# The S5 preparation rebuilt: tables from coarse times fine angles, K_n products issued together, their tile zeroed once, inputs loaded a tile ahead

## The chip, the cores and the metric

The kernel runs on one core of one Trainium2 chip. The metric is the device time of one execution in microseconds (us). Engines are named as in the profile: PE is TensorE's matmul, DVE is VectorE, ACT is ScalarE, POOL is GpSimd, SP is SyncE, which here only issues DMA transfers.

## The reference, cut to what matters

One step of a decoder of four layers on 256 prompt tokens and 8 samples of 4 tokens, 1024 features. Every layer has a token mixer and a squared-ReLU MLP. Layers 0 and 3 mix by a spatial gating unit, layer 1 by an RG-LRU, layer 2 by an S5 state-space layer:

```
h = rmsnorm(x, norm_mix[layer])
x = x + mixer(h)                                     # layer 0: gating unit, 1: RG-LRU, 2: S5
x = x + square(relu(rmsnorm(x, norm_ffn[layer]) @ w_ff1)) @ w_ff2
# S5, 64 groups of 16 features and 64 complex states:
ab = exp(lam * dt)                                   # lam = lam_re + i lam_im, dt = exp(log_dt)
bb = (ab - 1) / lam * B
x_t = ab * x_(t-1) + bb u_t ;  y_t = Re(C x_t) + d_skip * u_t ;  out = glu(gelu(y))
```

## The kernel before

Activations stay on chip as tiles of 128 features by 288 tokens. Every float32 product runs as three passes over split operands, weights whi and wlo against xh and xl (lines 273 to 275). The weights come as 176 chunks of 1 MB (`raw`), 44 per layer: 12 for the mixer of layer 0 (chunks 0 to 11), 32 for its MLP (12 to 43), and so on. A chunk is loaded by SP (line 179), split by ACT (whi, line 202) and DVE (wlo, line 203), and used on PE by 16 products of each of the three lines. Three raw buffers and three split buffers let the loads run some four chunks ahead. Each engine takes its instructions in order, and SP its DMA issues; a tile framework fixes that order at build time by priorities and by its own idea of times.

The S5 layer needs matrices that depend on weights alone. They are made while layers 0 and 1 run, as a list of background tasks that `spare` takes one by one, at a priority 300 steps later than their place. `s5_params` computes a, its powers (pw), q = (a − 1)/lambda, the cosines and sines of the angle times 4, 8 .. 128 (rc, rs), and a^(3−l) q (qq). `s5_spread` transposes qq on PE through two PSUM banks of the kind `sec` (there are three) and stores it to DRAM (qd). Then, for each of eight u tiles m, six tasks: `s5_inputs` twice (bi, on POOL, from bt and the spread qb), `s5_powers` twice (cn, on DVE), `s5_table` (tab, on POOL, 64 cosines and sines by doubling, 26 instructions), and `s5_kernels` (bq on DVE; eight small products into pk on PE, line 881; the copies of their blocks into the zeroed tile kt on ACT). Results go to DRAM (scr) and are fetched in layer 2. The tasks of four tiles run beside the MLP of layer 0, those of the other four beside that of layer 1. Within the mixer of layer 0, the tasks above `n_tasks` run while the u half of its first product is made:

```
def spare(upto=0):
    if len(background) > (upto or 0):
        with tc.high_priority(offset=-PRI_SPARE):
            background.pop(0)(state['bg'])
```

In the gating unit of layer 0 the rows after the u chunks are, for each of eight g: mixing products into a `sec` bank on PE (lines 508, 509), a scaled sum q on DVE (line 511), y = q * u on POOL (line 513), its split yh on ACT and yl on DVE (lines 269, 270), and then the output product.

## Time and profile before

| | |
|---|---|
| median of three runs | 1320.63 us (1314.42 to 1326.06) |
| profiled execution, span from the first to the last instruction | 1312.3 us; what lies around the span is not recorded |
| PE busy | 1266.0 us |
| mean granted clock of PE | 0.981 |
| HBM read and written | 214.17 and 14.60 MB |

PE is the engine with the most busy time; DVE is busy for 926.8 us, ACT for 617.9, POOL for 376.4. A busy PE isn't PE at its peak, since the ends of matmuls are modelled. Idle time of an engine matters only where another waits for it.

### The profile page before, as it was taken

The numbers are of one execution on the slowest core, as the hardware profiler recorded it, in microseconds if no ns is written. First come the engines' busy times: TensorE is split into PE (matmuls) and PEld (weight loads), VectorE is DVE, ScalarE is ACT, GpSimd is POOL, SyncE is SP. The second block draws the span as 40 slices with busy tenths as digits, with TensorE's granted clock in tenths as the row PEclk, the third lists the DMA queues.
The fourth block names the chain that finished last, engine by engine and source line by source line (L and its number), as shares of the span: only waits on it lengthen the run. The fifth ranks groups of instructions, "written<-read, shape, count | busy, mean of one in ns | idle before, by whom it ended". The sixth has DMA issues, their size and how long they took to land.

```text
span 1312.3 us, 23910 instructions
## 1 busy us (share of the span) xinstructions
PE 1266.0 (96%) x9802; PEld 1223.4 (93%) x9802; DVE 926.8 (71%) x1437; ACT 617.9 (47%) x1019; POOL 376.4 (29%) x524
## 2 busy tenths in 40 slices
PE   8999999799979998999999999999999999999997
PEld 7999999699968997998999899999999999999997
DVE  8899759686787897748768756655666677655653
ACT  5745532354564644236443345534544645534541
POOL 2237647501258485860121200000012221000010
PEclk9999999899988998999999999999999999999998
DMA  8526666555431767546567434554446334544431
GB/s 290 207 97 205 225 185 220 181 197 194 145 121 62 232 214 243 185 153 217 182 241 257 159 131 159 177 176 162 161 161 217 135 133 160 190 161 160 161 129 37
DMA packets 47006, 230.33 MB, mean 176 GB/s; under 512 B 7904, under 2 KB 13712, under 8 KB 24368
## 3 DMA queue, kind: packets, MB, share of 16 engines
q1 hardware_dynamic: 38016, 209.63, 46.5%
q0 software_dynamic: 8016, 18.45, 4.4%
q8 instruction: 77, 1.26, 0.4%
q10 hardware_dynamic: 864, 0.72, 0.2%
q14 instruction: 33, 0.27, 0.1%
HBM read 214.17 MB, written 14.60 MB: 174 GB/s over the span
## 4 chain that ended last, share of the span: by engine, by line
PE 63%; POOL 14%; DMA 9%; DVE 8%; issue 2%; ACT 2%; SPq 0%; DVEq 0%; POOLq 0%; ACTq 0%
PE acc L275 19%; PE acc L273 19%; PE acc L274 19%; DMA qb<-qd 6%; DMA scr<-tab 3%; POOL tab L905 2%; DVE wlo L203 2%; POOL ta L903 2%; POOL tab L904 2%; POOL bi L836 2%; POOL tb L903 1%; POOL bt L837 1%; POOL bi L838 1%; PE sec L959 1%; PE sec L881 1%
## 5 line engine op out<-in xcount | busy, mean ns | idle before, releaser
L202 ACT ACTIVATE whi<-raw 128x1024 fp32r<-128x1024 f32 (+1 forms) x354 | 363.6, 1048 | 330.9 <-PE acc L274 267.0
L203 DVE TENSOR_TENSOR wlo<-raw,whi 128x1024 fp32r<-128x1024 f32 (+1 forms) x354 | 443.4, 1269 | 106.4 <-ACT whi L202 104.6
L273 PE MATMUL acc<-xh,whi 128*128 128x288 f32 x1472 | 442.3, 301 | 8.0 <-ACT whi L202 7.1
L275 PE MATMUL acc<-xh,wlo 128*128 128x288 f32 x1472 | 440.1, 300 | 7.1 <-DVE wlo L203 7.0
L274 PE MATMUL acc<-xl,whi 128*128 128x288 f32 x1472 | 434.4, 295 | 2.1 <-DVE xl L285 2.1
L273 PE MATMUL acc<-hh,whi 128*128 128x288 f32 x1024 | 305.5, 298 | 3.9 <-ACT hh L269 3.9
L274 PE MATMUL acc<-hl,whi 128*128 128x288 f32 x1024 | 304.7, 298 | 1.1 <-DVE hl L270 1.1
L275 PE MATMUL acc<-hh,wlo 128*128 128x288 f32 x1024 | 303.2, 296 | 0.0
L273 PEld LDWEIGHTS acc<-xh,whi 128*128 128x128 f32 x1472 | 278.6, 189 | 12.5 <-ACT whi L202 8.1
L275 PEld LDWEIGHTS acc<-xh,wlo 128*128 128x128 f32 x1472 | 277.7, 189 | 11.8 <-DVE wlo L203 10.1
L274 PEld LDWEIGHTS acc<-xl,whi 128*128 128x128 f32 x1472 | 282.2, 192 | 5.9 <-DVE xl L285 3.4
L297 POOL TENSOR_TENSOR ss<-ss,sq 128x288 f32<-128x288 f32 x62 | 67.7, 1092 | 566.5 <-ACT sq L296 566.0
L273 PEld LDWEIGHTS acc<-hh,whi 128*128 128x128 f32 x1024 | 192.6, 188 | 7.3 <-ACT hh L269 4.7
L274 PEld LDWEIGHTS acc<-hl,whi 128*128 128x128 f32 x1024 | 192.9, 188 | 4.5 <-issue 2.6
L275 PEld LDWEIGHTS acc<-hh,wlo 128*128 128x128 f32 x1024 | 193.6, 189 | 2.4 <-issue 2.2
L411 DVE TENSOR_TENSOR t<-acc,r 128x288 f32<-128x288 f32 x64 | 29.1, 455 | 138.8 <-PE acc L275 138.8
L269 ACT ACTIVATE hh<-t 128x288 fp32r<-128x288 f32 x128 | 56.9, 444 | 125.6 <-DVE t L394 125.6
L270 DVE TENSOR_TENSOR hl<-t,hh 128x288 fp32r<-128x288 f32 x128 | 63.3, 495 | 25.8 <-ACT hh L269 24.4
L394 DVE TENSOR_TENSOR t<-t 128x288 f32<-128x288 f32 x128 | 64.8, 506 | 4.7 <-ACT t L388 4.7
L388 ACT ACTIVATE t<-acc 128x288 f32<-128x288 f32 x128 | 51.0, 398 | 21.8 <-PE acc L275 18.1
L285 DVE SCALAR_TENSOR_TENSOR xl<-x,aux,xh 128x288 fp32r<-128x288 f32 x64 | 52.9, 834 | 7.3 <-ACT xh L284 7.3
L284 ACT ACTIVATE xh<-x,aux 128x288 fp32r<-128x288 f32 x64 | 33.5, 527 | 33.9 <-DVE x L519 15.5
(324 smaller groups left out, 1508.1 us busy)
## 6 DMA issues: line engine op xcount, KB each, us to landing
raw<-in_wall SPq DMA_DIRECT2D x173, 1024.0 KB, 4.8
sci<-scr SPq DMA_DIRECT2D x8, 768.0 KB, 6.3
sco<-scr SPq DMA_DIRECT2D x8, 768.0 KB, 5.6
bt<-in_bt POOLq DMA_DIRECT2D x8, 512.0 KB, 7.7
scr<-cn SPq DMA_DIRECT2D x8, 512.0 KB, 5.0
qb<-qd POOLq DMA_DIRECT2D x8, 512.0 KB, 13.4
scr<-bi POOLq DMA_DIRECT2D x8, 512.0 KB, 6.1
raw<-in_wall SPq DMA_DIRECT2D x4, 512.0 KB, 8.9
```

The costliest lines, as they stand in the source:

```text
L202: nc.scalar.activation(h[:, c], self.raw[i][:, c], AF.Copy)
L203: nc.vector.tensor_tensor(l[:, c], self.raw[i][:, c], h[:, c].bitcast(F32), op=OP.subtract)
L269: S.activation(h, src, AF.Copy)
L270: V.tensor_tensor(l, src, h.bitcast(F32), op=OP.subtract)
L273: PE.matmul(ps, wh, h, start=first, stop=False)
L274: PE.matmul(ps, wh, l, start=False, stop=False)
L275: PE.matmul(ps, wl, h, start=False, stop=last)
L285: V.scalar_tensor_tensor(xl[k], x[k], A[g][:, k:k + 1], xh[k].bitcast(F32), op0=OP.mult, op1=OP.subtract)
L297: G.tensor_tensor(state['ss'], state['ss'], q, op=OP.add)
L388: i = S.activation(q, ps[:, :T], AF.Relu)
L394: V.tensor_tensor(q2, q, q, op=OP.mult)
L903: eng.tensor_tensor(t[:, :, :, :w], tab[:, :, :, :w], fb, op=OP.mult)
```

## The change

The diff also strips the comments from the file, so that line numbers move (L881 becomes L909, L513 becomes L515). What is left, cut to its core:

```diff
-  ... ('rc', [6, 32]), ('rs', [6, 32]), ('pw', [5, 3, 32]), ('q', [2, 32]), ('qq', [4, 32, 2])
+  ... ('fine', [2, 32, 8]), ('coarse', [2, 32, 8]), ('pw', [5, 3, 32]), ('q', [2, 32])
 def s5_params(pool):
...
-        V.tensor_copy(s5['rs'].rearrange('p n i -> p (n i)'), sn[:, 64:])
-        V.tensor_copy(s5['rc'].rearrange('p n i -> p (n i)'), cs[:, 64:])
+        rc, rs = (v[:, 64:].rearrange('p (n i) -> p n i', n=6) for v in (cs, sn))
+        fine, coarse = s5['fine'], s5['coarse']
+        G.tensor_copy(fine[:, 0, :, 0], rc[:, 0])
+        G.tensor_copy(fine[:, 1, :, 0], rs[:, 0])
+        G.memset(coarse[:, 0, :, 0], 1.0)
+        G.memset(coarse[:, 1, :, 0], 0.0)
+        ta, tb = (pool.tile([P, 2, 32, 4], F32, name=f's5d{i}') for i in range(2))
+        for tab, first in ((fine, 0), (coarse, 3)):
+            for n in range(3):
+                w = 2 ** n
+                for t, f in ((ta, rc), (tb, rs)):
+                    G.tensor_tensor(t[:, :, :, :w], tab[:, :, :, :w], f[:, first + n][:, None, :, None].to_broadcast([P, 2, 32, w]), op=OP.mult)
+                G.tensor_tensor(tab[:, 0, :, w:2 * w], ta[:, 0, :, :w], tb[:, 1, :, :w], op=OP.subtract)
+                G.tensor_tensor(tab[:, 1, :, w:2 * w], ta[:, 1, :, :w], tb[:, 0, :, :w], op=OP.add)
+    def s5_loads(m):
+        four = slice(4 * m, 4 * m + 4)
+        bt, qb = bg_([P, 2, 4, P], 'bt', 2), bg_([P, 4, 2, P], 'qb', 2)
+        cc, bs = bg_([P, 2, 4, 32], 'cc', 2), bg_([P, 2, 4, 32], 'bs', 2)
+        nc.sync.dma_start(qb...)      # the same transfers; bt and qb were issued by POOL,
+        nc.sync.dma_start(bt, ...)    # cc and bs by SP in s5_powers and s5_kernels
+        nc.sync.dma_start(cc, ...)
+        nc.sync.dma_start(bs, ...)
+        s5['in', m] = bt, qb, cc, bs
 def s5_inputs(m, n, eng):
         if n == 0:
+            if m == 0 or m == KT // 2:
+                s5_loads(m)
+                s5['kt'] = bg_([P, 4, P], 'kt')
+                G.memset(s5['kt'], 0.0)
...
 def s5_powers, s5_kernels:      # the stores of cn and kt
-            nc.sync.dma_start(s5['scr'][m][:, 1536:2560]..., cn...)
+            G.dma_start(s5['scr'][m][:, 1536:2560]..., cn...)
-        nc.sync.dma_start(s5['scr'][m][:, 2560:3072], ...kt)
+        G.dma_start(s5['scr'][m][:, 2560:3072], ...kt)
 def s5_kernels(m, eng):
-        for n in range(2):
+        lead = None
+        for n in (1, 0):
             for q in range(4):
-                PE.matmul(pk[32 * q:32 * q + 32, :P], bq[:, n, q], cn[:, n, 0:4, q], start=n == 0, ...)
+                with ExitStack() as stay:
+                    if lead is not None:
+                        stay.enter_context(tc.high_priority())
+                        stay.enter_context(tc.issue_after(lead.ins))
+                    i = PE.matmul(pk[32 * q:32 * q + 32, :P], bq[:, n, q], cn[:, n, 0:4, q], start=n == 1, ...)
+                lead = lead or i
-        kt = bg_([P, 4, P], 'kt')
-        G.memset(kt, 0.0)
+        kt = s5['kt']
...
-            S.activation(kt[s, :, s], pk[s, :P]..., AF.Copy)
+            # blocks 1 and 3 so on ACT; blocks 0 and 2 by V.tensor_copy on DVE
 def s5_table(m, eng):            # six instructions in place of 26
+        for c in range(2):
+            fine = s5['fine'][:, c, four][:, :, None].to_broadcast([P, 4, 8, 8])
+            for t, n in ((ta, 0), (tb, 1)):
+                step = s5['coarse'][:, n, four][:, :, :, None].to_broadcast([P, 4, 8, 8])
+                eng.tensor_tensor(t[:, c]..., fine, step, op=OP.mult)
+        eng.tensor_tensor(tab[:, 0], ta[:, 0], tb[:, 1], op=OP.subtract)
+        eng.tensor_tensor(tab[:, 1], ta[:, 1], tb[:, 0], op=OP.add)
-        n_tasks[0] = 6 * KT + 1
+        n_tasks[0] = 6 * KT
-  lambda p, m=m_: s5_inputs(m, 0, G)
+  lambda p, m=m_: (s5_inputs(m, 0, G), (m + 1) % (KT // 2) and s5_loads(m + 1))
```

With `n_tasks` one lower, `s5_spread` now runs in the mixer of layer 0 with `s5_params`, and not in the MLP.

What stands where in a row is shown at three places. First, PE in the MLP of layer 0, at the K_n products of the second tile of 128 (`sec<-cn,bq`; the main products of the MLP are `acc<-xh,whi` and the like). Before:

```order
L275 MATMUL acc_2928<-xh_95,wlo_2809 128x288
L881 MATMUL sec_2532<-cn_2237,bq_2524 32x128
L273 MATMUL acc_2928<-xh_96,whi_2808 128x288
L881 MATMUL sec_2532<-cn_2237,bq_2524 32x128
L274 MATMUL acc_2928<-xl_104,whi_2808 128x288
L881 MATMUL sec_2532<-cn_2237,bq_2524 32x128
L275 MATMUL acc_2928<-xh_96,wlo_2809 128x288
```

Now:

```order
L275 MATMUL acc_2834<-xh_97,whi_2740 128x288
L276 MATMUL acc_2834<-xl_105,whi_2740 128x288
L909 MATMUL sec_2468<-cn_2193,bq_2460 32x128 x8
L277 MATMUL acc_2834<-xh_97,wlo_2741 128x288
L275 MATMUL acc_2834<-xh_98,whi_2740 128x288
```

The eight products of a tile, which alternated with the main products, stand in one run; all eight tiles read so now.

Second, the gating unit of layer 0, where its u chunks end and its mixing begins. PE before (`vT`: the transposed v; `wr`, `wrs`: the mixing weights):

```order
L274 MATMUL acc_1029<-xl_106,whi_953 128x288
L275 MATMUL acc_1029<-xh_98,wlo_954 128x288
L508 MATMUL sec_1106<-wr_218,vT 128x128
L508 MATMUL sec_1106<-wr_219,vT 128x128
L509 MATMUL sec_1106<-wrs,vT 128x32
```

PE now (`s5qq` is what `s5_spread` transposes):

```order
L276 MATMUL acc_1067<-xl_106,whi_991 128x288
L277 MATMUL acc_1067<-xh_98,wlo_992 128x288
L833 MATMUL sec_981<-ident,s5qq 128x128
L833 MATMUL sec_986<-ident,s5qq 128x128
L510 MATMUL sec_1144<-wr_217,vT 128x128
L510 MATMUL sec_1144<-wr_218,vT 128x128
L511 MATMUL sec_1144<-wrs,vT 128x32
```

The two transposes of the spread stand ahead of the first mixing product. POOL at the same place before (`ss<-ss,sq` adds up the squares of the norm, L513 is y):

```order
L466 TENSOR_TENSOR ss_304<-ss_304,sq_555 128x288
L466 TENSOR_TENSOR ss_304<-ss_304,sq_572 128x288
L492 DMA out_vs<-vo 32x1024
L513 TENSOR_TENSOR t_77_1112<-t_1110,u_221 128x288
L513 TENSOR_TENSOR t_80_1122<-t_1120,u_222 128x288
```

POOL now, the last of the new instructions (L784 and the lines about it are `fine` and `coarse`):

```order
L784 TENSOR_TENSOR s5coarse<-s5d_812,s5d_813 128x32x2
L782 TENSOR_TENSOR s5d_812<-s5coarse,s5w_789 128x256
L782 TENSOR_TENSOR s5d_813<-s5coarse,s5w_788 128x256
L783 TENSOR_TENSOR s5coarse<-s5d_812,s5d_813 128x32x4
L784 TENSOR_TENSOR s5coarse<-s5d_812,s5d_813 128x32x4
L515 TENSOR_TENSOR t_79_1150<-t_1148,u_220 128x288
```

The 26 instructions of the two tables' parts stand ahead of the first y (L515, formerly L513).

Third, SP's queue in the MLP of layer 0. `raw` are the weight chunks: `raw_1672` before and `raw_1719` now are chunk 18, `raw_1749` and `raw_1794` chunk 19. Before:

```order
L179 DMA raw_1587<-in_wall 128x2048
L847 DMA cc_2678<-in_cc 128x2x128
L863 DMA scr_114<-cn_1742 128x2x512
L179 DMA raw_1672<-in_wall 128x2048
L179 DMA raw_1749<-in_wall 128x2048
L871 DMA bs_2993<-in_bs 128x2x128
L179 DMA raw_1824<-in_wall 128x2048
```

Now:

```order
L848 DMA bs_1631<-in_bs 128x2x128
L844 DMA qb_2116<-qd 128x1x1024
L181 DMA raw_1719<-in_wall 128x2048
L846 DMA bt_2115<-in_bt 128x2x512
L844 DMA qb_2549<-qd 128x1x1024
L181 DMA raw_1794<-in_wall 128x2048
L847 DMA cc_2117<-in_cc 128x2x128
L846 DMA bt_2548<-in_bt 128x2x512
L181 DMA raw_1869<-in_wall 128x2048
```

The loads of qb for tiles 2 and 3 of 128 (`qb_2116`, `qb_2549`) stand ahead of chunks 18 and 19 in one queue; in the MLP of layer 1 two such loads stand ahead of chunks 63 and 65.

## Rows read from the trace of the kernel before

**Rows 1.** The page's first part: busy time of each engine, its share and instructions.

```profile
PE 1266.0 (96%) x9802; PEld 1223.4 (93%) x9802; DVE 926.8 (71%) x1437; ACT 617.9 (47%) x1019; POOL 376.4 (29%) x524
```

**Rows 2.** Windows, L273 alone: window, length, PE, PEld, granted clock, DMA share, GB/s.

```profile
104.00:337.90 233.90, 154.08 (x513) 97.19 (x513) 0.98 0.60 197
440.90:674.40 233.50, 153.85 (x513) 96.84 (x513) 0.99 0.60 197
801.40:1005.90 204.50, 151.66 (x513) 96.13 (x513) 1.00 0.48 166
...
104.00:150.50 46.50, 33.17 (x112) 1.00 0.65 219
```

**Rows 3.** Timeline of PE, start and duration: single L881, then a run with five.

```profile
610.85 0.29 PE L275 MATMUL acc<-xh,wlo 128*128 128x288 f32 x1
611.08 0.41 PE L881 MATMUL sec<-cn,bq 128*32 128x128 f32 x2
...
616.44 0.29 PE L273 MATMUL acc<-xh,whi 128*128 128x288 f32 x1
...
572.79 0.40 PE L275 MATMUL acc<-xh,wlo 128*128 128x288 f32 x1
573.12 0.62 PE L881 MATMUL sec<-cn,bq 128*32 128x128 f32 x10
...
573.91 0.30 PE L274 MATMUL acc<-xl,whi 128*128 128x288 f32 x1
```

**Rows 4.** Waits of PE: who waited for what; us in total, times, longest.

```profile
PE acc L273 <- ACT whi L202: 9.2, 3, 6.6
PE acc L275 <- DVE wlo L203: 7.6, 12, 1.2
PE acc L273 <- ACT hh L269: 3.9, 3, 1.9
```

**Rows 5.** Timelines of ACT and POOL about 250 us; in brackets the wait ahead.

```profile
253.27 1.11 ACT L887 ACTIVATE kt<-sec 32x128 f32<-32x128 f32 x4 [11.87 <-POOL kt L884]
...
244.09 1.29 POOL L836 TENSOR_TENSOR bi<-bt,qb 128x512 f32<-128x512 f32 x1 [5.58 <-DMA qb<-qd]
```

**Rows 6.** Window behind that wait: length, PE busy, clock, DMA share, GB/s.

```profile
255.80:262.00 6.20, 5.78 (x22) 0.50 0.57 187
```

**Rows 7.** Groups of POOL by form: busy, mean ns, idle time before.

```profile
L836 POOL TENSOR_TENSOR bi<-bt,qb 128x512 f32<-128x512 f32 x16 | 25.0, 1563 | 56.3 <-DMA qb<-qd 56.3
L903 POOL TENSOR_TENSOR ta<-tab,s5rc 128x256 f32<-128x256 f32 x8 | 8.2, 1020 | 0.5
L903 POOL TENSOR_TENSOR tb<-tab,s5rs 128x256 f32<-128x256 f32 x8 | 6.0, 752 | 0.0
```

**Rows 8.** Timelines of PE and POOL where layer 0's u chunks end.

```profile
70.13 0.29 PE L275 MATMUL acc<-xh,wlo 128*128 128x288 f32 x1
...
71.98 2.45 POOL L513 TENSOR_TENSOR t<-t,u 128x288 f32<-128x288 f32 x2 [14.05 <-DVE t L511]
```

**Rows 9.** The page's fifth part, the group of L203.

```profile
L203 DVE TENSOR_TENSOR wlo<-raw,whi 128x1024 fp32r<-128x1024 f32 (+1 forms) x354 | 443.4, 1269 | 106.4 <-ACT whi L202 104.6
```

**Rows 10.** Timelines of POOL and DVE at the parameters, layer 0.

```profile
87.31 0.81 POOL L297 TENSOR_TENSOR ss<-ss,sq 128x288 f32<-128x288 f32 x1 [4.30 <-ACT sq L296]
...
87.43 0.74 DVE L750 TENSOR_TENSOR s5w<-s5w 128x32 f32<-128x32 f32 x1
...
88.53 0.18 DVE L751 TENSOR_TENSOR s5mag<-s5w 128x32 f32<-128x32 f32 x1
88.63 0.18 DVE L775 TENSOR_TENSOR s5pw<-s5w,s5w 128x32 f32<-128x32 f32 x1
...
93.88 0.41 DVE L766 TENSOR_TENSOR s5w<-s5w 128x256 f32<-128x256 f32 x1
```

**Rows 11.** Timeline of SP's queue: two weight loads issued together.

```profile
122.33 7.05 SPq L179 DMA_DIRECT2D raw<-in_wall  x2
```

**Rows 12.** DMA issues, weights: count, KB each, median us from issue to landing.

```profile
raw<-in_wall SPq DMA_DIRECT2D x173, 1024.0 KB, 4.8
```

More of the change, by code (lines that the diff above doesn't have):

```diff
@@ L7 @@
+from contextlib import ExitStack
 import numpy as np
@@ L729, in body @@
     if 2 in layers:
-        for n, shape in (('mag4', [32]), ('s0', [2, 32, NB]), ('rc', [6, 32]), ('rs', [6, 32]), ('pw', [5, 3, 32]), ('q', [2, 32]), ('qq', [4, 32, 2])):
+        for n, shape in (('mag4', [32]), ('s0', [2, 32, NB]), ('fine', [2, 32, 8]), ('coarse', [2, 32, 8]), ('pw', [5, 3, 32]), ('q', [2, 32])):
             s5[n] = persist.tile([P] + shape, F32, name=f's5{n}')
@@ L806, in s5_params @@
         V.tensor_tensor(qi, qi, den, op=OP.mult)
-        qq = s5['qq']
+        qq = s5['qq'] = pool.tile([P, 4, 32, 2], F32, name='s5qq')
         V.tensor_copy(qq[:, 3, :, 0], qr)
@@ L845, in s5_powers @@
         if d == 0:
-            s5['cc'] = bg_([P, 2, 4, 32], 'cc', 2)
-            nc.sync.dma_start(s5['cc'], a['cc'][:, :, four])
             s5['cn'] = bg_([P, 2, 5, 4, 32], 'cn')
-        cc, cn = s5['cc'], s5['cn']
+        cc, cn = s5['in', m][2], s5['cn']
         t1 = bg_([P, 5, 4, 32], 'ct1')
@@ L862, in s5_powers @@
         if d == 1:
[L863 to L864 removed]
+            G.dma_start(s5['scr'][m][:, 1536:2560].rearrange('p (d n c) -> p d n c', d=2, n=4),
+                        cn[:, :, 1:].rearrange('p d n q f -> p d n (q f)'))
     def s5_kernels(m, eng):
@@ L869, in s5_kernels @@
         cn = s5['cn']
-        bs = bg_([P, 2, 4, 32], 'bs', 2)
-        nc.sync.dma_start(bs, a['bs'][:, :, four])
+        bs = s5['in', m][3]
         bq = bg_([P, 2, 4, 32], 'bq')
@@ L885, in s5_kernels @@
+        kt = s5['kt']
         for q in range(4):
             s = slice(32 * q, 32 * q + 32)
-            S.activation(kt[s, :, s], pk[s, :P].rearrange('p (n f) -> p n f', n=4), AF.Copy)
+            if q % 2:
+                S.activation(kt[s, :, s], pk[s, :P].rearrange('p (n f) -> p n f', n=4), AF.Copy)
+            else:
+                V.tensor_copy(kt[s, :, s], pk[s, :P].rearrange('p (n f) -> p n f', n=4))
         V.scalar_tensor_tensor(kt[:, 0], ident, A['d_skip'][:, m:m + 1], kt[:, 0], op0=OP.mult, op1=OP.add)
-        nc.sync.dma_start(s5['scr'][m][:, 2560:3072], kt.rearrange('p n f -> p (n f)'))
+        G.dma_start(s5['scr'][m][:, 2560:3072], kt.rearrange('p n f -> p (n f)'))
@@ L891, in s5_table @@
     def s5_table(m, eng):
-        tab = bg_([P, 2, 4, NBL], 'tab')
-        ta = bg_([P, 2, 4, 32], 'ta')
-        tb = bg_([P, 2, 4, 32], 'tb')
+        tab, ta, tb = (bg_([P, 2, 4, NBL], n) for n in ('tab', 'ta', 'tb'))
         four = slice(4 * m, 4 * m + 4)
-        eng.tensor_copy(tab[:, 0, :, 0], s5['rc'][:, 0, four])
-        eng.tensor_copy(tab[:, 1, :, 0], s5['rs'][:, 0, four])
-        for n in range(6):
-            w = 2 ** n
-            for t, f in ((ta, s5['rc']), (tb, s5['rs'])):
-                fb = f[:, n, four][:, None, :, None].to_broadcast([P, 2, 4, w])
-                eng.tensor_tensor(t[:, :, :, :w], tab[:, :, :, :w], fb, op=OP.mult)
-            eng.tensor_tensor(tab[:, 0, :, w:2 * w], ta[:, 0, :, :w], tb[:, 1, :, :w], op=OP.subtract)
-            eng.tensor_tensor(tab[:, 1, :, w:2 * w], ta[:, 1, :, :w], tb[:, 0, :, :w], op=OP.add)
+        for c in range(2):
+            fine = s5['fine'][:, c, four][:, :, None].to_broadcast([P, 4, 8, 8])
+            for t, n in ((ta, 0), (tb, 1)):
+                step = s5['coarse'][:, n, four][:, :, :, None].to_broadcast([P, 4, 8, 8])
+                eng.tensor_tensor(t[:, c].rearrange('p q (i j) -> p q i j', j=8), fine, step, op=OP.mult)
```

22 lines of the change are left out of this document (10 added, 12 removed).

## The prediction

> **What bounds the kernel now.** I read the page first: PE is busy for 1266.0 of 1312.3 us [rows 1], so a gain has to come out of PE's idle time, its half-clock time or its own instructions. Second, the stretches by stage [rows 2]: each MLP is 32 weight chunks of 16 L273 products. The MLP of layer 2 has no side work and takes 204.5 us, 6.39 us a chunk; those of layers 0 and 1, beside which the S5 preparation runs, take 233.9 and 233.5. So 29.4 + 29.0 = 58.4 us is all that the preparation costs PE there, and the ceiling of any gain. Third, PE's timeline shows what the 58 us are.
>
> Most is the K_n products (L881). They stand one by one between main products [rows 3]. Main products follow each other every 0.133 us (a chunk's 48 in 6.39), but from 610.85 to 616.44 eight L881 products and ten main steps take 5.59 us, so the eight cost 5.59 − 1.33 = 4.26 us. Six of the eight tiles look like that; in the other two some stand together already, and they cost 3.2 and 2.35. Sum 31.1 us. The rest is idle time [rows 4]: PE waits for weight splits (L202, L203) and for the MLP's activation splits (L269). The longest wait, 6.6 us before 255.8, goes back by the timelines of ACT and POOL [rows 5]: ACT stands 11.87 us before a copy into kt, whose zeroing is on POOL, and POOL has stood 5.58 us for qb. When PE resumes, its granted clock is 0.50, the level of 1.2 GHz, for 6.2 us [rows 6], and 22 products take 5.8 us instead of 2.9: 2.9 us lost.
>
> **The products together.** In all eight tiles the eight products are now one run on PE. The trace has no run of eight; it has one of five [rows 3]: from the main product at 572.79 to the one at 573.91 is 1.12 us where two steps would take 0.27, so five cost 0.85. Bounds for eight: 0.85, and 8/5 of it, 1.4; I take 1.1, since part of the 0.85 is going in and out. Six tiles gain 4.26 − 1.1, the others 2.1 and 1.25: **−22 us** (−20 to −24), on PE, which is the path here.
>
> **The zeroed tile.** kt is zeroed once for four tiles, so ACT no longer waits for POOL's zeroing: the 6.6, some 0.4 behind it, and 2.9 of clock: **−10 us**. Next is the store of the tile before, which the copies must still wait for; a tile comes every 40 us or so, and the store is long done, so nothing.
>
> **POOL and the smaller waits.** A table costs 26 instructions on POOL now; the new one has six of 256 elements, at 0.75 to 1.02 us [rows 7], 0.89 on average, 5.3 in all. POOL is not on PE's path by itself, but it slows DVE, and in layer 1's MLP PE waits 3.9 us for hh [rows 4] and loses some 2 more at half clock. POOL stays busy there for the first 45 us, only with other work, so I take half: **−3 us** (0 to −6). Short waits on L203 in both MLPs, of the 7.6 in [rows 4]: **−3 us**.
>
> **The tables' base, and the spread, in layer 0's mixer.** This is a price that the diff doesn't show. Some 70 DVE instructions of the parameters are left when the mixer's last u is done, and they fill gaps until 109. In the new order they all stand on DVE ahead of the first mixed row (L513, formerly L511), because the spread's two transposes stand on PE ahead of the mixing products, whose PSUM banks they use; and 26 POOL instructions (fine and coarse) stand ahead of the products y (L515, formerly L513). Now PE ends the u chunk at 70.13 + 0.29 and POOL starts y at 71.98 [rows 8]. Newly, from 71.4, DVE has two halves of a split, 1.2 each when nothing holds them and 1.27 on average [rows 9], 2.4; five instructions of 256 elements, at 0.41 or less [rows 10], 1.8; and 68 of 32 elements. These issue every 0.10 us when free [rows 10] and at about 0.2 when each needs the last; at 0.13 they are 8.7. With 0.5 for Sin on ACT, DVE alone would be through at 71.4 + 12.9 + 0.5 = 84.8. POOL needs the cosines, which come after the split, the five and 18 small ones: 78.4. Its two chains have 12 instructions each, from 64 to 256 elements; at 0.6, between the old table's small forms (0.25) and its longest [rows 7], they are 15, so POOL is done at 94 (at 0.4: 88.5). Beside a POOL addition of 0.81 us a DVE multiplication that takes 0.18 took 0.74 [rows 10]: it waited for POOL to end. With 24 POOL instructions in a row, each holds back one small DVE instruction, and DVE too ends near 95. Then two transposes, two copies, a mixed row, y: y starts at 96 (89 to 101) instead of 71.98. PE stands still meanwhile and comes back at half clock, another 2.9: **+27 us** (20 to 32). Nothing covers it: DVE gets its gaps after 96 back, but PE was not waiting for DVE there.
>
> Here a rule bears on the sum. The Trainium skill, SBUF — State Buffer, section "Who interferes with whom", says that a DVE instruction with two SBUF inputs and a GpSimd one that reads SBUF exclude each other for a whole instruction. The one pair in [rows 10] agrees. By the rule the stall is the 27; if it held for none of the small ones, y would wait for POOL alone and the term would be 20.
>
> **Loads a tile ahead.** bt, qb, cc and bs of the next tile go to SP, where the weights are. Each new qb needs the buffer of two tiles before, so it waits until POOL's bi has read that one. In the new order the load of qb for tile 2 stands on SP ahead of weight chunk 18, and qb for tile 3 ahead of chunk 19; formerly these two chunks left at 122.33 and 7 us behind [rows 11], and nothing of POOL's held them. I count from T0 = 104.0, the MLP's first product. POOL can begin at about T0 + 5.5, when the preparation's first loads leave now. Until tile 1's last reading of qb it has one memset (0.5), 22 table instructions at 0.89, 11 of bi at 1.5 [rows 7], one addition (1.1), four DMA issues (2.4) and about 1 us for a table's store to land: 41.1, so T0 + 46.6. SP's queue then moves qb and the chunk, 1.5 MB at 4.8 us per MB [rows 12], 7.2, and the split takes 2.3 or more: T0 + 56. PE needs chunk 19 at T0 + 46.5 [rows 2] (the row with x112). That is 9.5 us, and 2.9 of clock: **+12 us** (2 if POOL takes the short ends and starts earlier, 21 if bi takes 1.8). The later chunks aren't held and catch up. In layer 1 the same two loads stand ahead of chunks 63 and 65, with POOL's bi some 20 and 6 us further ahead of need: **+2** (0 to 6). That qb no longer stops POOL is in the count, since I let bi begin when the tables are done.
>
> **The sum** against the profiled span of 1312.3: −22 −10 −3 −3 +27 +12 +2 = **+3 us**. The page gives no more than the span for that execution; the median of the three runs, 1320.63, is 8.3 above it, and carried over that makes 1324. About 1% (13 us) is what a measurement can tell from no change: the three runs lie from 1314 to 1326.
>
> **Rivals.** *The mixer's stall is short and the queue doesn't matter* (0.20): DVE's small instructions slip between POOL's, y waits for POOL at its short times (+20), tile 1's products end before T0 + 38 (+2, and nothing in layer 1), and layer 1's wait for hh goes wholly (−6): −22 −10 −6 −3 +20 +2 = −19, **1302**. For it: bi has taken 1.29 us [rows 5]; against it: the means in [rows 7], and [rows 10]. *The weights wait behind the tile loads* (0.20, the slower side): every microsecond by which POOL ends tile 1 after T0 + 37 is one of PE. If bi takes 1.8 us and a table instruction 1.1, the end is T0 + 54 and chunk 19 costs 18 + 2.9; chunks 63 and 65 cost 6 + 2.9; the wait for hh stays: −22 −10 −3 +27 +21 +9 = +22, **1343**. It decides from about T0 + 50 on. *The products together cost what they cost apart* (0.05), because each still has the array changed for it: of the −22 some −4 is left, +21, **1342**. Against it: the run of five.
>
> **How the numbers follow.** No change, 1324, has 0.55. From 1303 to 1343 the range holds all of that and the near parts of the first and second rival; what it leaves out is the far ends of these, some 0.2. Faster by over 1% is the first rival, 0.20; slower is the second and third, 0.25.
>
> **What would show it.** After the change: L909 in eight runs of about 1.1 us; no wait of ACT before kt; a hole on PE of some 25 us from 70.4, ended by the transposes and by POOL's y; a second hole near chunk 19, with a weight load that left just behind a qb load; the MLPs of layers 0 and 1 at about 224 and 214 us. I am wrong if the first hole is under 15 us, or if no weight load is late.

## The result, and the profile after

The changed kernel takes 1355.24 us (median of four runs, 1354.13 to 1359.23), the kernel before 1323.14 in the same comparison: a ratio of 1.0266, with a 95% interval of 1.0227 to 1.0306. It is 2.7% slower, above the predicted range. The profiled span grew from 1312.3 to 1352.3 us.

The stages, from first main product to first main product, in us:

| stage | before | after | difference | predicted |
|---|---|---|---|---|
| mixer, layer 0 | 97.4 | 122.2 | +24.8 | +27 |
| MLP, layer 0 | 233.9 | 243.3 | +9.4 | about −10 |
| mixer, layer 1 | 103.0 | 102.8 | −0.2 | 0 |
| MLP, layer 1 | 233.5 | 242.3 | +8.8 | about −19 |
| mixer, layer 2 | 127.1 | 125.6 | −1.5 | 0 |

The mixer's total came out as forecast. The two MLPs, which I had at 224 and 214 us, a gain of 29, lost 18.2. An MLP makes its first product (w_ff1) for half of the hidden features in chunks 1 to 8, its second (w_ff2) in 9 to 16, and both for the other half in 17 to 32 (counted within the MLP). Here are the windows of these parts after, for the MLP of layer 0 and then of layer 1. The columns are the window, its length, the busy time (instructions) of PE, PEld, DVE, ACT and POOL, the granted clock, the DMA share and GB/s.

```profile
128.50:206.10 77.60, 59.76 (x388) 57.59 (x386) 63.44 (x53) 23.29 (x41) 64.13 (x59) 0.89 0.67 198
206.10:267.50 61.40, 55.90 (x402) 53.83 (x401) 40.78 (x59) 22.83 (x30) 2.71 (x4) 0.94 0.55 188
267.50:371.80 104.30, 104.30 (x818) 103.22 (x817) 76.80 (x118) 51.79 (x84) 10.42 (x11) 1.00 0.53 180
474.60:549.30 74.70, 59.87 (x388) 57.77 (x386) 73.22 (x59) 25.16 (x46) 64.58 (x60) 0.86 0.66 208
549.30:612.70 63.40, 56.38 (x402) 53.75 (x402) 42.95 (x59) 22.82 (x30) 6.25 (x6) 0.95 0.54 184
612.70:716.90 104.20, 104.20 (x817) 103.12 (x817) 76.79 (x118) 51.80 (x84) 10.42 (x11) 1.00 0.53 179
```

And the first two parts of each before:

```profile
104.00:157.20 53.20, 52.33 (x391) 51.55 (x390) 48.48 (x95) 29.68 (x52) 37.49 (x65) 1.00 0.65 219
157.20:211.60 54.40, 54.40 (x403) 52.33 (x402) 36.87 (x40) 18.00 (x22) 32.92 (x58) 1.00 0.65 201
440.90:494.80 53.90, 52.23 (x387) 51.28 (x387) 52.15 (x61) 26.46 (x47) 40.91 (x46) 1.00 0.71 220
494.80:558.70 63.90, 58.88 (x402) 54.56 (x401) 47.28 (x55) 22.03 (x31) 41.66 (x56) 0.95 0.64 210
```

The last 16 chunks take 104.3 and 104.2 us; the four windows of before leave 126.3 and 115.7 of its MLPs for them. There the gain is: 33.5 us. The first eight chunks take 77.6 and 74.7 in place of 53.2 and 53.9, the next eight 61.4 and 63.4 in place of 54.4 and 63.9: 51.7 us lost. In these four windows PE's waits for wlo, the lower halves of the split weights, are 31.9 us (0.7 before). The granted clock adds to that: its means of 0.89, 0.94, 0.86 and 0.95 are worth up to 25.5 us (3.4 before), an estimate by (1 − clock) × length that overlaps with the waits, since PE also stands still at half clock. In the first eight, POOL is now busy for 64 us, where it was for 37 and 41, and nearly all of POOL's preparation stands there. PE's waits, answering to [rows 4] (who waited for what; us in total, times, longest):

```profile
PE acc L277 <- DVE wlo L205: 36.2, 21, 5.4
PE sec L833 <- DVE s5qq L800: 16.7, 2, 16.3
PE acc L275 <- ACT hh L271: 7.1, 6, 2.0
```

The first is the new one in the MLPs, 7.6 us in the whole kernel before. The second is the mixer's hole. The groups of DVE by form in the first eight chunks of the MLP of layer 0, after (busy, mean ns, idle time before):

```profile
L205 DVE TENSOR_TENSOR wlo<-raw,whi 128x1024 fp32r<-128x1024 f32 x13 | 25.0, 1921 | 1.0 <-ACT whi L204 1.0
L272 DVE TENSOR_TENSOR hl<-t,hh 128x288 fp32r<-128x288 f32 x11 | 14.3, 1299 | 1.0 <-ACT hh L271 1.0
L396 DVE TENSOR_TENSOR t<-t 128x288 f32<-128x288 f32 x11 | 12.8, 1167 | 0.0
...
L318 DVE RECIPROCAL r<-ms 128x288 f32<-128x288 f32 x1 | 1.9, 1939 | 0.0
```

and before:

```profile
L203 DVE TENSOR_TENSOR wlo<-raw,whi 128x1024 fp32r<-128x1024 f32 x17 | 21.3, 1255 | 2.0 <-ACT whi L202 2.0
L394 DVE TENSOR_TENSOR t<-t 128x288 f32<-128x288 f32 x15 | 8.1, 538 | 0.0
L270 DVE TENSOR_TENSOR hl<-t,hh 128x288 fp32r<-128x288 f32 x15 | 7.4, 491 | 2.0 <-ACT hh L269 2.0
...
L316 DVE RECIPROCAL r<-ms 128x288 f32<-128x288 f32 x1 | 1.9, 1940 | 0.0
```

The instructions are the same and last longer: a chunk has two of each of the first three, 2 × (1.26 + 0.54 + 0.49) = 4.6 us before and 2 × (1.92 + 1.30 + 1.17) = 8.8 after, and PE wants a chunk every 6.4. The reciprocal, with one input, lasts as long as ever.

The products together read as the prediction said. PE's timeline of the changed kernel, start and duration:

```profile
279.57 0.29 PE L276 MATMUL acc<-xl,whi 128*128 128x288 f32 x1
279.80 0.64 PE L909 MATMUL sec<-cn,bq 128*32 128x128 f32 x16
280.37 0.40 PE L277 MATMUL acc<-xh,wlo 128*128 128x288 f32 x1
280.61 0.29 PE L275 MATMUL acc<-xh,whi 128*128 128x288 f32 x1
```

From 279.57 to 280.61 is 1.04 us for two main steps (0.27) and the eight products: these cost 0.77, in all eight tiles. The wait for POOL's zeroing before kt's copies [rows 5] is gone. ACT now waits there for DVE's copies of the other two blocks (L918), 17.4 us in eight waits, the longest 4.2; PE's longest wait for whi is 2.4. In the mixer PE waits from 70.3 to 86.62, POOL's first y starts at 89.92, and the clock then stays at 0.50, the level of 1.2 GHz, for 17.4 us (timelines of PE, POOL, and a window of the engines):

```profile
86.62 0.45 PE L833 MATMUL sec<-ident,s5qq 128*128 128x128 f32 x1 [16.34 <-DVE s5qq L800]
89.92 0.79 POOL L515 TENSOR_TENSOR t<-t,u 128x288 f32<-128x288 f32 x1
86.60:104.00 17.40, 17.03 (x61) 14.47 (x62) 7.86 (x21) 3.53 (x8) 9.60 (x15) 0.50 0.03 8
```

And the weight load that I expected to be late is late: SP's queue in the MLP of layer 0, chunk 19 at 175.96, 47.5 us after the MLP's first product (I had 46.6), right behind qb:

```profile
175.30 0.57 SPq L844 DMA_DIRECT2D qb<-qd  x1
175.96 0.42 SPq L181 DMA_DIRECT2D raw<-in_wall  x1
```

So two suspects stand in the same place: this queue (theory Q), and POOL holding DVE (theory L in the first experiments). The experiments start there. Each result is a median in us, with its ratio to the kernel before and the 95% interval of that; the kernel before, timed beside each group of runs, had medians of 1318.4 to 1322.2. Differences to the changed kernel are taken from its 1355.24.

### The profile page after: what moved, and what is told of

Same layout as the page of the kernel before. It is cut to its first block, busy times and chain, and to the rows that moved or that the text cites. A ratio compares the mean times of both kernels' runs of the same rounds, so it can differ in the third digit from the quotient of the medians.

```text
span 1352.3 us, 23756 instructions
## 1 busy us (share of the span) xinstructions
PE 1261.7 (93%) x9802; PEld 1231.6 (91%) x9802; DVE 954.3 (71%) x1451; ACT 615.5 (46%) x1003; POOL 322.2 (24%) x386
## 3 DMA queue, kind: packets, MB, share of 16 engines
q8 instruction: 77, 1.26, 0.4%
## 4 chain that ended last, share of the span: by engine, by line
PE 55%; DVE 7%; issue 1%; ACT 1%; POOL 0%; DVEq 0%; ACTq 0%
PE acc L275 17%; PE acc L277 17%; PE acc L276 17%; DVE wlo L205 3%; PE sec L986 1%; DVE hl L272 1%; DVE t L396 1%; PE acc L978 1%; PE acc L1024 1%; PE acc L1028 1%; ACT whi L204 0%; DVE yl L272 0%; DVE t L513 0%; PE sec L471 0%; PE sec L909 0%
## 5 line engine op out<-in xcount | busy, mean ns | idle before, releaser
L205 DVE TENSOR_TENSOR wlo<-raw,whi 128x1024 fp32r<-128x1024 f32 (+1 forms) x354 | 459.3, 1315 | 116.1 <-ACT whi L204 114.2
L277 PE MATMUL acc<-xh,wlo 128*128 128x288 f32 x1472 | 445.3, 303 | 32.8 <-DVE wlo L205 32.7
L277 PEld LDWEIGHTS acc<-xh,wlo 128*128 128x128 f32 x1472 | 282.1, 192 | 38.6 <-DVE wlo L205 37.3
L275 PEld LDWEIGHTS acc<-xh,whi 128*128 128x128 f32 x1472 | 283.1, 192 | 6.5 <-ACT t L390 3.8
L276 PEld LDWEIGHTS acc<-xl,whi 128*128 128x128 f32 x1472 | 286.2, 194 | 2.4 <-DVE xl L287 1.4
L413 DVE TENSOR_TENSOR t<-acc,r 128x288 f32<-128x288 f32 x64 | 29.3, 457 | 152.5 <-PE acc L277 152.3
L272 DVE TENSOR_TENSOR hl<-t,hh 128x288 fp32r<-128x288 f32 x128 | 74.0, 578 | 25.4 <-ACT hh L271 23.4
L396 DVE TENSOR_TENSOR t<-t 128x288 f32<-128x288 f32 x128 | 70.5, 550 | 4.8 <-ACT t L390 4.6
L390 ACT ACTIVATE t<-acc 128x288 f32<-128x288 f32 x128 | 51.2, 400 | 24.8 <-PE acc L277 24.7
L920 POOL DMA_DIRECT2D scr<-kt x8 | 4.5, 560 | 201.5 <-DVE kt L919 201.5
```

Source lines behind the costliest of these rows:

```text
L205: nc.vector.tensor_tensor(l[:, c], self.raw[i][:, c], h[:, c].bitcast(F32), op=OP.subtract)
L272: V.tensor_tensor(l, src, h.bitcast(F32), op=OP.subtract)
L275: PE.matmul(ps, wh, h, start=first, stop=False)
L276: PE.matmul(ps, wh, l, start=False, stop=False)
L277: PE.matmul(ps, wl, h, start=False, stop=last)
L390: i = S.activation(q, ps[:, :T], AF.Relu)
```

## The experiments

### Which of the two makes the splits late

**a_no_reload.** In the changed kernel:

```diff
 def s5_loads(m):
+    if m % (KT // 2) > 1:
+        s5['in', m] = s5['in', m - 2]
+        return
```

> The changed kernel, but tiles 2, 3, 6 and 7 of the preparation use the inputs of tiles 0, 1, 4 and 5 again and load none of their own (their matrices are then those of the wrong tile). So no weight load stands behind a load of qb any more, while POOL's work stays the same. Theory Q (weight chunks are held on SP behind qb until POOL has read its buffer): PE's waits for wlo fall from 36.2 us to under 15, the MLPs of layers 0 and 1 from 485.6 us together to about 460, and the time from 1355 to about 1330. Theory L (in the new order POOL's instructions follow each other without a break, and a DVE instruction with two SBUF inputs only starts when POOL has a break, so that the splits of the weights are late): waits for wlo stay above 28 us and the time within 8 us of 1355.

1355.87 (ratio 1.0271, 1.0230 to 1.0311): no change. PE waited 47.2 us for wlo; the first eight chunks took 84.5 and 82.1, the next eight 54.0 and 58.0, and the two MLPs 487.1 together. So Q is not what makes this kernel slow. The traces say why. A load also needs the raw buffer of the third chunk before, which DVE's split of that chunk frees. In the changed kernel the splits of chunks 15 and 16 ended at 160.31 and 171.51, and chunks 18 and 19 left at 160.38 and 175.96: qb held the first not at all and the second 4.4 us. Here the same splits ended at 159.22 and 170.43, and the loads left at 159.28 and 170.50. And ACT and DVE came to these chunks later still: in the changed kernel chunk 18 had landed at 170.55, and ACT split it from 188.51, behind an hh that waited for DVE; chunk 19 was split from 195.42. The edit also moves POOL's work a little, so a cost of a few us that this hides isn't excluded.

**a_order**, POOL's bi and table instructions each issued after the one written before it:

```diff
+    def after(f, *args, **kw):
+        with ExitStack() as stay:
+            if last:
+                stay.enter_context(tc.issue_after(last[-1].ins))
+            last.append(f(*args, **kw))
-        eng.tensor_tensor(bi[:, n], bt[:, 0], qb[:, :, n], op=OP.mult)
+        after(eng.tensor_tensor, bi[:, n], bt[:, 0], qb[:, :, n], op=OP.mult)
...
```

> The changed kernel, with POOL's bi and table instructions held in the order in which they are written: three of bi, three of bi, six of the table, tile after tile. No instruction is added or removed; an instruction that needs the one right before it now comes every two to four instructions, and in the trace such a pair has a break of 0.08 us. Theory L: unbroken runs on POOL are at most 5 us long instead of 13, waits for wlo fall from 36.2 us to 10 to 25, and the time by 10 to 25, to some 1330 to 1345. Theory Q: qb of a tile is read earlier or later by a few us only, so within 8 us of 1355. Theory W (DVE simply has too much work in the first half of these MLPs): within 8 us of 1355.

1358.85 (1.0292, 1.0263 to 1.0322). A miss for L: the longest record of a split on DVE fell from 13.52 us to 3.93, but PE's waits for wlo stayed at 35.2 and the time did not fall.

**a_gaps**, the same and one-element copies between:

```diff
+            if was is not None:
+                after(eng.tensor_copy, t[:, c, 0, 0:1], was)
+            was = t[:, c, 3, NBL - 1:NBL]
             after(eng.tensor_tensor, t[:, c]..., fine, step, op=OP.mult)
...
```

> As the kernel with POOL's order held, and between two POOL instructions that don't depend on each other a copy of one element that makes the second wait for the first (six more POOL instructions per tile). POOL has more work, not less, and a break behind nearly every instruction. Theory L: a DVE instruction waits for one POOL instruction at most; waits for wlo fall from 36.2 us to under 12, the MLPs of layers 0 and 1 to some 445 to 455 us together, the time to 1318 to 1330. Theory Q: POOL reads qb later, weights are held longer: 1355 to 1370. Theory W: 1355.

1344.73 (1.0188, 1.0158 to 1.0218): 10.5 less than the changed kernel, where L asked for 25 or more. Waits for wlo fell to 18.6, those for hh rose to 13.2. Beside the first eight chunks POOL was busy for 55.8 and 48.9 us, where it was for 67.0 and 62.2 in a_order, and beside the next eight for 25.5 and 34.7 in place of 1.3 and 11.7. So the copies both made breaks and moved part of POOL's work to another place, and how the gain divides between the two isn't shown.

**a_all_dve**:

```diff
-  s5_inputs(m, 0, G) ... s5_inputs(m, 1, G) ... s5_table(m, G)
+  s5_inputs(m, 0, V) ... s5_inputs(m, 1, V) ... s5_table(m, V)
```

> The changed kernel, with all of bi and the tables computed by DVE in place of POOL. DVE gets 48 instructions of 512 elements (about 0.65 us each, from 0.81 for 640 elements) and 48 of 256 (0.36): some 49 us more in the two MLPs, and POOL nearly nothing. Theory L: DVE is never held, waits for wlo fall under 10 us, the MLPs to some 430 to 445 us together, the time to 1300 to 1320. Theory W: DVE has 25 us more to do in each MLP's first half, so waits for wlo rise above 36 us and the time above 1360. Theory Q: the loads of qb wait for DVE in place of POOL, no better than 1345.

1306.80 (0.9901, 0.9872 to 0.9930): 48.4 less, and below the kernel before, with 96 instructions more on DVE. The first eight chunks took 52.7 and 56.4, PE waited 5.8 us for wlo. DVE's amount of work (W) is refuted; that the work stands on POOL, beside DVE, is the cause. DVE's groups in those eight chunks of layer 0:

```profile
L205 DVE TENSOR_TENSOR wlo<-raw,whi 128x1024 fp32r<-128x1024 f32 x14 | 16.9, 1214 | 0.0
L396 DVE TENSOR_TENSOR t<-t 128x288 f32<-128x288 f32 x13 | 5.8, 443 | 0.0
L272 DVE TENSOR_TENSOR hl<-t,hh 128x288 fp32r<-128x288 f32 x12 | 5.4, 448 | 0.0
```

### How POOL holds DVE: breaks, amount or place

**m_run, m_chain, m_second**: a block of 24 POOL multiplications in the kernel before, in the MLP of layer 2, which has no other side work.

```diff
+  for i in range(24):      # m_run and m_second; m_second copies one column of hh[15] into ex[6] first
+      G.tensor_tensor(ex[i % 6], ex[6], ex[7], op=OP.mult)
+  for i in range(24):      # m_chain
+      G.tensor_tensor(ex[i % 2], ex[1 - i % 2], ex[7], op=OP.mult)
```

> The disputed cost by itself: the kernel before, and in the MLP of layer 2, which has no side work and takes 204.5 us, POOL multiplies two constant tiles of 512 elements 24 times, none needing another's result: one unbroken run of some 30 us. Theory L: a DVE instruction with two SBUF inputs that is due in the run waits for nearly all of it, one record of DVE reads 20 us or more, PE runs out of split weights (its wait for wlo 10 us or more), and this MLP takes 218 to 235 us. Theory one-by-one (as in my prediction: each DVE instruction waits only for the POOL instruction that is running): no DVE record over 3 us, and the MLP takes 205 to 212.

> The same with each of the 24 multiplications reading the result of the one before, so that POOL has a break between any two. Theory L and theory one-by-one agree here: no DVE record over 3 us, the MLP of layer 2 takes 205 to 212 us. If POOL's mere busy time beside DVE counts, as much as in the unbroken run.

> The kernel before, with the 24 independent multiplications of POOL in the MLP of layer 2 again, but held until the last hh of the first half is made, so that they run beside the second product. Theory T: there a chunk has only three DVE instructions with two SBUF inputs (two wlo, one addition to x), 2.9 us free and some 6.2 held, under the chunk's 6.4; this MLP takes 205 to 209 us, where it took 215.2 with the same work beside the first product. Theory V (POOL's work costs the same wherever it stands): 213 to 217.

The MLP of layer 2 took 215.2 us with m_run and 215.5 with m_chain, against 204.5: in this block breaks make no difference, and no record of DVE there is over 2.4 us. With a_order, L falls as the account of the loss. With m_second it took 204.5: beside the second product the same block is free. Each is one run, but this MLP took 204.4 or 204.5 us in every other kernel of this document. (The whole times, 1338.8, 1330.4 and 1311.8, say little, since other stages differ more: the MLP of layer 0, which has no edit, took 242.1, 245.6 and 235.8 us, with a wait of PE behind kt, 6.6 us in [rows 4], of 16.9, 19.5 and 11.1.) Windows of the engines in m_run (the first eight chunks) and in m_second (while the block ran):

```profile
816.00:873.40 57.40, 53.74 (x388) 52.80 (x387) 51.06 (x44) 25.70 (x45) 44.68 (x33) 0.97 0.37 124
```

```profile
855.00:899.00 44.00, 44.00 (x333) 44.00 (x332) 39.06 (x28) 14.06 (x14) 43.45 (x24) 1.00 0.47 158
```

POOL's groups of the 24, in m_run and in m_second:

```profile
L407 POOL TENSOR_TENSOR ex<-ex,ex 128x512 f32<-128x512 f32 x24 | 39.9, 1699 | 0.1
```

```profile
L410 POOL TENSOR_TENSOR ex<-ex,ex 128x512 f32<-128x512 f32 x24 | 43.6, 1855 | 0.1
```

And what DVE did beside them, in m_run:

```profile
L203 DVE TENSOR_TENSOR wlo<-raw,whi 128x1024 fp32r<-128x1024 f32 x7 | 15.7, 2246 | 0.0
L394 DVE TENSOR_TENSOR t<-t 128x288 f32<-128x288 f32 x8 | 11.9, 1484 | 1.1 <-ACT t L388 1.1
L270 DVE TENSOR_TENSOR hl<-t,hh 128x288 fp32r<-128x288 f32 x7 | 8.9, 1278 | 1.1 <-ACT hh L269 1.1
```

and in m_second:

```profile
L203 DVE TENSOR_TENSOR wlo<-raw,whi 128x1024 fp32r<-128x1024 f32 x13 | 29.6, 2312 | 0.0
L419 DVE TENSOR_TENSOR x<-x,t 128x288 f32<-128x288 f32 x7 | 7.2, 1036 | 0.2
L418 DVE TENSOR_TENSOR t<-acc,r 128x288 f32<-128x288 f32 x7 | 3.2, 458 | 4.7 <-PE acc L275 4.7
```

In both, every DVE instruction with two SBUF inputs lasts longer, in turn with POOL: the split 2.25 and 2.31 us where it takes 1.22 free, the others 1.04 to 1.48 where they take about 0.45. L418 reads one of its inputs from PSUM and isn't held (458 ns). The first product has six held instructions a chunk, 2 × (2.25 + 1.48 + 1.28) = 10.0 us, more than the 6.4 that PE leaves; the second has three, 2 × 2.31 + 1.04 + 0.46 = 6.1. That is theory T: DVE and POOL take turns, and what the work on POOL costs depends on how many such DVE instructions a chunk has where it stands. By m_second the place decides; theory V, the same price everywhere, had 213 to 217. The Trainium skill, SBUF — State Buffer, section "Who interferes with whom", says that a DVE instruction contends with a GpSimd one that reads SBUF if it has two SBUF inputs, and not if it has at most one and is outside the 2-port modes; these rows agree (L419 at 1036 ns, L418 at 458).

**a_late**, a first try at moving POOL's work in time in the changed kernel:

```diff
-                if m % 2:
+                if m % 2 and st['half']:
                     spare(upto)
```

> The changed kernel, with no preparation task started beside the first eight chunks of the MLPs of layers 0 and 1 (first product, first half); the 24 tasks follow in the same order beside the other 24 chunks. Theory T (while POOL works without pause, each DVE instruction with two SBUF inputs first waits for the POOL instruction that is running, some 1.1 us; the first product has six such instructions a chunk, 4.2 us of its 6.4 when free, 10.8 when held, the second only four, 3.3 when free, 7.7 when held): the first eight chunks take 53 us in place of 77.6 and 74.7, the next eight 62 to 70 each, the time falls to 1315 to 1335. Theory V (POOL's work costs PE the same wherever it stands): the loss moves along, within 8 us of 1355.

1372.14 (1.0414, 1.0375 to 1.0453). It did not move what it was to move: POOL was busy for 19.7 of the 20 us from 150 to 170, as in the changed kernel: the edit changes the tasks' place in the program, and nothing that POOL waits for. Only the last tasks became later, and the mixers of layers 1 and 2 took 8.0 and 11.9 us more. It tells nothing between T and V.

**a_gate**, with POOL itself held until the second product begins:

```diff
+                after(G.tensor_copy, s5['kt'][:, 0, 0:1], state['hh'][15][:, 0:1].bitcast(F32))
+                after(G.memset, s5['kt'], 0.0)
...
                     spare(upto)
+                    if not half:
+                        spare(upto)
```

(also the order of a_order and the line of a_late)

> The changed kernel, with all of POOL's bi and tables held, by a copy from the last hh of the first half, until the second product begins; two tasks a chunk there, so that the preparation ends where it did. The run before it moved the tasks in the program and not on POOL: POOL did its work as early as ever. Theory T: the first eight chunks take 52 to 55 us in place of 77.6 and 74.7, the next eight 54 to 64, and the time falls to 1310 to 1330. Theory V: the loss of 24 us moves into the second product, within 8 us of 1355. If the held qb loads now stop the weights on SP (my theory Q, at a later place), above 1340.

1312.82 (0.9957, 0.9930 to 0.9984): 42.4 less than the changed kernel, with all of POOL's work still on POOL. The first eight chunks took 52.6 and 51.6, the next eight 60.1 and 57.0 (51.2 in layer 2, where nothing runs beside). V is refuted. The windows of layer 0's first and next eight:

```profile
128.60:181.20 52.60, 51.75 (x388) 51.29 (x387) 37.94 (x61) 27.50 (x47) 2.15 (x3) 1.00 0.72 219
181.20:241.30 60.10, 54.65 (x386) 53.83 (x385) 37.16 (x36) 17.89 (x21) 53.61 (x47) 0.94 0.67 205
```

What is lost in the second is Q after all, once DVE isn't later: qb loads left at 196.43 and 212.89, each with a chunk behind it (197.74 and 214.18), and the split on ACT waits for these weights. ACT's timeline at 214 and 230:

```profile
214.49 2.01 ACT L204 ACTIVATE whi<-raw 128x1024 fp32r<-128x1024 f32 x2 [11.51 <-DMA raw<-in_wall]
230.32 2.00 ACT L204 ACTIVATE whi<-raw 128x1024 fp32r<-128x1024 f32 x2 [13.83 <-DMA raw<-in_wall]
```

and PE stood 4.8 and 3.2 us for whi, one for each MLP.

**a_bi_dve**, the edit of a_all_dve for bi alone.

> The changed kernel with bi on DVE and the tables still on POOL. POOL's work in each MLP falls from 64 to about 25 us. Theory T: POOL holds DVE for 25 us in place of 64, of which the two chunks that are split ahead cover most: 1306 to 1320. If it is the tables (four independent instructions in a row) that hold DVE and not bi, above 1335. If bi on DVE is too much for it, above 1355.

1327.64 (1.0060, 1.0034 to 1.0087): 27.6 less than the changed kernel, 20.8 more than with the tables on DVE as well, and between the forecasts, above T's 1306 to 1320. The first eight chunks took 58.7 and 57.8. Both kinds of work count, but the 20.8 aren't told apart: the tables on POOL still held DVE (in those chunks its split took 1.29 and 1.40 us on average, 1.21 and 1.23 in a_all_dve), and with bi on it DVE stood up to 5.5 us for bt and PE waited 17.1 us for hh, up to 8.9 at once.

### The mixer, and the edits alone

**a_spread_mlp**: the spread and the base of the tables as tasks of the MLP, with rc, rs and qq kept until then.

```diff
-        n_tasks[0] = 6 * KT
+        n_tasks[0] = 6 * KT + 1
 def s5_spread(pool):
+    rc, rs = s5['rc'], s5['rs']
+    fine, coarse = s5['fine'], s5['coarse']
+    G.tensor_copy(fine[:, 0, :, 0], rc[:, 0])
...
```

> The changed kernel, with the spread and the 26 instructions of fine and coarse moved out of layer 0's mixer into the MLP of layer 0, where the spread stood in the kernel before; POOL still does bi and the tables. If the mixer's stall comes from the transposes and the base standing ahead of the mixing (my step of +27), the mixer of layer 0 goes back from 122.2 to 97 to 100 us. The MLP of layer 0 gets POOL's 26 instructions (some 13 us) and starts bi later, and by theory L it loses up to 10 us more. Together 1335 to 1345, from 1355. If the stall comes from the parameters on DVE alone, wherever the spread stands, the mixer stays above 115.

1325.96 (1.0073, 1.0043 to 1.0104): 29.3 less. The mixer took 97.7, as before the change, and nothing of the stall came back in the MLP of layer 0 (236.3 us, 7 less, where I had up to 10 more). POOL's work there starts later, so that 39.7 us of it stand beside chunks 9 to 16 and 43.9 beside 1 to 8, where it was 2.7 and 64.1: as T has it, the second place is the cheaper one.

**a_dve_spread**: that edit and a_all_dve, fine and coarse on DVE too.

> The two remedies together: spread, fine and coarse in the MLP, and all of bi, tables, fine and coarse on DVE. If the two causes are separate places, the gains add: 1306.8 less 23 for the mixer, plus 0 to 8 for what the MLP takes over: 1284 to 1292, which is 2 to 3% below the kernel before. If the stall of the mixer only moves into the MLP, 1300 to 1308.

1286.37 (0.9767, 0.9733 to 0.9801): 68.9 less than the changed kernel, where the two alone give 77.7 together.

**a_gate_spread**: the edits of a_gate and a_spread_mlp together.

> The same with spread, fine and coarse in the MLP of layer 0 as well. If the mixer's stall and POOL's work beside the first product are the two causes of the slowdown, with both removed the gains of the grouped products and the zeroed tile are left: 1285 to 1305, below the kernel before. POOL's 26 instructions for fine and coarse then still run beside the first product of layer 0 and may cost up to 6 of it.

1313.48 (0.9971, 0.9945 to 0.9997), a miss: no better than a_gate. The mixer took 97.8, but in the MLP of layer 0 POOL now stood until 225.9 for the first qb, and its work fell beside the other first product: chunks 17 to 24 took 86.3 us in place of 52.3. POOL's timeline:

```profile
225.91 1.61 POOL L865 TENSOR_TENSOR bi<-bt,qb 128x512 f32<-128x512 f32 x1 [63.85 <-DMA qb<-qd]
```

**a_dve_late**: a_dve_spread with the line of a_late.

> The fastest so far of the changed kernel (spread in the MLP, everything on DVE, 1286) with the tasks kept out of the first eight chunks. There is nothing on POOL to hold DVE, but DVE's queue is long where the first product ends and the second begins, and PE waits there for hh. If that backlog is the preparation's, the wait goes and the time falls to 1272 to 1282. If it only moves to the next such place, 1283 to 1292.

1309.22 (0.9931, 0.9904 to 0.9959), a miss, 22.9 more: the last tasks ran into the mixers of layers 1 and 2, which took 9.5 and 12.1 us more than in a_dve_spread. In the MLP of layer 0 chunks 9 to 16 did fall from 65.5 to 52.0 us, but 17 to 32 rose from 104.3 to 119.0.

**b_together** and **b_kt**: one edit each in the kernel before.

```diff
-        for n in range(2):
+        lead = None
+        for n in (1, 0):
             for q in range(4):
-                PE.matmul(pk..., start=n == 0, stop=n == 1)
+                with ExitStack() as stay:      # as in the change
...
```

> The kernel before, with the one edit that a tile's eight K_n products are issued together. My step of -22: 1296 to 1304, with L881 in eight runs that cost PE about 1.1 us each. If the products cost together what they cost apart, within 4 us of 1322.

```diff
         if n == 0:
+            if m == 0 or m == KT // 2:
+                s5['kt'] = bg_([P, 4, P], 'kt')
+                G.memset(s5['kt'], 0.0)
...
-        kt = bg_([P, 4, P], 'kt')
-        G.memset(kt, 0.0)
+        kt = s5['kt']
```

> The kernel before, with the one edit that kt is zeroed once for four tiles. My step of -10: 1309 to 1314, and no wait of 11.9 us on ACT before kt's copies, no wait of PE of 6.6 us for whi. If something else is late behind it (POOL's wait for qb, the products), within 3 us of 1322.

b_together: 1309.21 (0.9924, 0.9893 to 0.9956), 10 less and not 20, a miss. PE stood 24.5 us behind the copies into a kt that POOL had not zeroed. ACT came to them at 237.7, 3.7 us earlier than in the kernel before, and POOL zeroed kt at 264.2, 11.5 later, after it had stood 24.0 us for a qb (14.3 before). In the three runs with the block in layer 2, whose MLP of layer 0 has no edit, POOL stood 16.6 to 24.6 us for that qb and PE 11.1 to 19.5 behind kt, so how much of the 24.5 the edit makes isn't shown. The timelines of ACT and PE in it:

```profile
264.81 1.11 ACT L894 ACTIVATE kt<-sec 32x128 f32<-32x128 f32 x4 [27.12 <-POOL kt L891]
267.48 0.61 PE L274 MATMUL acc<-xh,whi 128*128 128x288 f32 x1 [24.46 <-ACT t L389]
```

b_kt: 1302.47 (0.9890, 0.9856 to 0.9925), 16.5 less by the medians where I had 10. PE's longest wait for whi fell to 2.7 us.

**b_tog_kt**: both.

> The kernel before with both edits, products together and kt zeroed once, with bi, tables, spread and loads as they were. Alone the first gave 10 and left a wait of 24.5 us on PE that goes back to kt, the second gave 17. If that wait was what hid the rest of the first, the two give 25 (of the products) and 17: some 1275 to 1283. If they share a gain, 1290 to 1300.

1287.20 (0.9758, 0.9730 to 0.9787): 31.5 less, between the two forecasts. The two alone give 26.3; with intervals of some 4 us on each, that doesn't tell a shared gain from a sum. On top of b_kt the products gain 15.3. It stands level with a_dve_spread, 2.4% and 2.3% below the kernel before.

**b_tog_kt_bidve**: b_tog_kt with bi on DVE.

> The same with bi on DVE as well. If POOL's bi (512 elements, up to 1.9 us each) still costs PE something there, 3 to 8 us less than without it. If DVE's added 30 us are what counts, 0 to 10 us more.

1347.03 (1.0218, 1.0190 to 1.0246), a miss, 59.8 more. DVE in its own order stands for the loads that POOL issues late, and the splits behind it; DVE's timeline:

```profile
187.91 0.69 DVE L840 TENSOR_TENSOR bi<-bt,qb 128x512 f32<-128x512 f32 x1 [31.65 <-DMA qb<-qd]
```

PE waited 55.7 us for hh. a_all_dve and a_dve_spread, which have the loads a tile ahead, don't have that: in these runs bi on DVE pays only with them.

## Why the prediction was wrong, step by step

**What bounds the kernel** held: PE, and in the two MLPs 58 us to be gained at most.

**The products together**, −22: right as a cost on PE, and somewhat more. Eight cost 0.77 us, not 1.1; 31.1 less 8 × 0.77 is −24.9. In time they gave 10 alone and 15 on top of b_kt; waits of PE take the rest, and these aren't accounted for one by one.

**The zeroed tile**, −10: right in kind, 16.5 alone. The hole of [rows 5] was a mild one: ACT stood 11.87 us there, and 19.9 to 27.6 in m_second, m_run, m_chain and b_together.

**POOL and the smaller waits**, −3 and −3: here the prediction failed. It was a loss of more than 40 us. I took fewer POOL instructions as relief for DVE and gave POOL's busy first 45 us in layer 1 half a gain. But the change fills POOL's pauses and lengthens its instructions. Before, bi stood still for 56.3 us for qb [rows 7], and most of the tables' instructions were short (0.2 to 0.4 us where nothing held them, 0.61 for 256 elements), so that DVE got through: by the windows above, 65 POOL instructions of 0.58 us on average in the first eight chunks of layer 0. After, the loads are there, and 59 instructions of 1.09 us make 64 us of POOL work in the 75 to 78 us of those chunks, just where DVE has six instructions a chunk with two SBUF inputs. The pair in [rows 10], a DVE multiplication that waited for a POOL addition, was before me; I used it for the mixer and not here. In the part on the loads I wrote that qb no longer stopping POOL "is in the count": it was in the count of the loads, and not in DVE's. The runs put the price at 42 us (a_gate) to 48 (a_all_dve). Roughly, the pieces make the whole: −31.5 for products and tile (b_tog_kt), +24.8 for the mixer and +42 to +48 are +35 to +41, and the medians differ by 32.1, the profiled spans by 40.0.

**Loads a tile ahead**, +12 and +2: chunk 19 left at 47.5 us where I had 46.6, but that match is luck: until 43.0 it waited for its raw buffer, which DVE's late split of chunk 16 freed, and only the last 4.4 us are qb's. The queue's price doesn't show in this kernel, since DVE was later. The mechanism is there: in a_gate it costs 4.8 and 3.2 us of PE's standing.

**The mixer**, +27: right in cause (a_spread_mlp: 97.7) and right in sum (24.8) by luck, since its two halves are wrong and make up for each other. POOL's chain began at 78.26 (I had 78.4), but its 24 instructions took 0.44 us on average and not 0.6, so it ended at 89.8 and not at 94. Beside it 20 of DVE's small instructions were held, by 0.2 us each, and DVE was through with the parameters at 87.2 and not near 95. So y started at 89.92 and not at 96. The clock was half for 17.4 us behind the hole, a loss of 8.7 and not 2.9; the hole of 16.3 and 8.7 make 25.

The rival on the slower side had its sign right and its mechanism wrong: it also blamed the queue.

What stays open is the exact share of bi and of the tables, since moving them to DVE also gives DVE waits of its own, and how much of the 10.5 us of a_gaps is due to the breaks.

## What to carry to other kernels

Two engines that take turns, as DVE and POOL do here, must be costed as one timetable: ask not how much work the idle engine loses but beside which of the other's instructions the rest will now stand. A wait can be a shield; before it is removed, name what the released engine will do in that time, and whom it holds. Test edits that share a path together as well as alone, because what an edit gives can hang on another: bi on DVE costs 59.8 us in b_tog_kt, and is part of a gain in the changed kernel, whose loads come earlier.
